# Issuing the paced conditioning loads from GpSimd instead of ScalarE in a two-layer diffusion backbone

## The chip, the core and the metric

The kernel runs on one core of one Trainium2 chip. The metric is device microseconds for one launch. Three runs of the kernel before gave 2462.93, 2460.25 and 2460.77 us (median 2460.77). One further execution was profiled: it took 2457.31 us, and the instructions in its trace span 2455.5 us.

The engines are named as the profile names them: PE (TensorE matmul) with PEld (its weight loads), DVE (VectorE), ACT (ScalarE), POOL (GpSimd) and SP (SyncE, which here only issues DMAs). Every engine runs its own instructions in the order that was fixed when the program was built.

## The reference

The model has two layers on 256 latent tokens (width 2048) with a prefix of 256 context tokens that is used in layer 0 only. Layer 0 mixes by attention (16 heads, a clamped 8 by 16 window of grid neighbours with a learned bias, and all context keys, in one softmax). Layer 1 mixes by a gated MLP with a 128 by 128 position matrix for each of 16 groups. A SwiGLU FFN of inner width 5632 follows each mixer. Cut to what matters:

```python
def ada_params(cond, w, b):
    return jnp.split(jax.nn.silu(cond) @ w + b, 6, axis=-1)
...
sh1, sc1, g1, sh2, sc2, g2 = ada_params(c[:, None, :], ada_w[i], ada_b[i])
a = modulate(h, sh1, sc1)                       # h * (1 + scale) + shift
...
h = layer_norm(ALPHA * h + g1 * y, ln_g[i, 0], ln_b[i, 0])
h = layer_norm(ALPHA * h + g2 * swiglu(modulate(h, sh2, sc2), ffn_w_in[i], ffn_w_out[i]),
               ln_g[i, 1], ln_b[i, 1])
```

For one conditioning vector, `silu(cond) @ w` is a product of a vector with a matrix of 2048 by 12288 in each layer. It has little arithmetic, but every byte of `ada_w` must come from memory. This document is about the loads of that matrix.

## The kernel before

**The matrix products.** Float32 operands are split into a high part `hi` and a rest `lo`, and each product is three matmuls (`mm3`, lines 89 to 91). Weights come in *pieces* of 128 by 1024 (512 KB): SP issues the load into one of four `raw` buffers, ACT casts it to `hi` (line 94, a tile `hw...`), and DVE subtracts to get `lo` (line 95, a tile `lw...`). In the FFN a product uses one piece for 12 matmuls of 512 columns, and up to five pairs of `hi` and `lo` exist, so four pieces can be ahead. In the attention stage there are three pairs, two ahead.

**The stages.** First come the modulated input, keys and values of the first heads (up to about 160 us), then the attention heads, the output projection, FFN of layer 0 (blocks named `pg`, `pu` and, for the way down, `pod`), the gated MLP (`gv`, `gu`, `pogo`), and FFN of layer 1.

**The paced conditioning work.** Most of `silu(c) @ ada_w` is not needed at once. It is cut into 320 tasks, each on one 128 by 1024 piece of `ada_w` (512 KB). A dot task (192 of them, load named `ad`, line 153) multiplies the piece by `silu(c)` and sums it along the row, for shifts and scales. A gate task (128 of them, load named `ag`, line 177) adds the scaled piece to a `gate` tile in place. Both are one DVE instruction, SCALAR_TENSOR_TENSOR. After 32 gate tasks a sum task has POOL add the `gate` tile over the partitions (line 192, PARTITION_ALL_REDUCE). `pace` and `tick` spread the tasks in the written program: after each piece, `tick` adds credit and runs as many tasks as it pays for. `fetch_ahead` writes the load of a task up to three tasks ahead of its use (`FETCH = 3`), and the loads share four buffers (`ADA = 4`), so a load waits until the DVE instruction of the task four before it is done.

**What sets the order.** A scheduler that builds the program takes the written instructions and fixes each engine's order. The written order is the priority, but an instruction that the scheduler takes to be ready early may be placed early on its engine. `keep_in_program_order` adds one rule: the instruction stays behind the instruction that was written just before it for the same engine. It says nothing on other engines.

POOL has little else to do: four memsets of `gate` tiles with a small DMA each (lines 171 and 172), the four sums of line 192, and broadcasts of norm rows over the partitions (line 83), each of which waits for a small SP load.

Of the kernel before, what the change touches and what calls it, by code (L numbers as in the profile page):

```python
# [52 lines left out]
def hybrid_kernel(ctx: ExitStack, tc: tile.TileContext, i, out):  # L53
    nc = tc.nc
# [20 lines left out]

    def load(src, name):
        r = outer.tile([P, 1024], F32, tag="ada", name=name, bufs=ADA)
        tc.keep_in_program_order(nc.scalar.dma_start(r, src))
        return r

    def spread(dst, src):
# [61 lines left out]
    def dot_task(layer, t, nt, half):  # L143
        key = (layer, t, nt, half)

        def fetch():
            src = i["ada_t"][dot_index(layer, t, nt)]
            loaded[key] = load(src[:, half * 1024 : (half + 1) * 1024], f"ad{layer}{t}{nt}{half}")

        def run():  # L150
            r = loaded.pop(key)
            o = (cols2 if half else cols)[:, layer, t, :]
            V.scalar_tensor_tensor(  # L153
                r, r, 1.0, c_bc[:, half * 1024 : (half + 1) * 1024], ALU.mult, ALU.mult,
                accum_out=o[:, nt : nt + 1],
            )
            if nt == KT - 1 and half:
                o = cols[:, layer, t, :]
                V.tensor_tensor(o, o, cols2[:, layer, t, :], ALU.add)
                V.tensor_tensor(o, o, badj[:, layer, t, :], ALU.add)  # L160
        return [(layer, t), 0.5, run, fetch]

    def gate_task(layer, t, kt, half):
        key = (layer, t, kt, half)
        sl = slice(half * 1024, (half + 1) * 1024)

        def fetch():
            if kt == 0 and half == 0:
                g = outer.tile([P, D], F32, tag="gate", name=f"gate{layer}{t}")
                gate[(layer, t)] = g  # L170
                nc.gpsimd.memset(g, 0.0)
                nc.gpsimd.dma_start(g[0:1, :], i["ada_b_row"][layer, t : t + 1, :])
            loaded[key] = load(i["ada_g"][gate_index(layer, t, kt)][:, sl], f"ag{layer}{t}{kt}{half}")

        def run():
            g = gate[(layer, t)][:, sl]
            V.scalar_tensor_tensor(g, loaded.pop(key), c_col[:, kt, 0:1], g, ALU.mult, ALU.add)  # L177
        return [(layer, t), 0.5, run, fetch]
# [826 lines left out]
```

## Time and profile before

| | |
|---|---|
| median of three runs | 2460.77 us (2460.25 to 2462.93) |
| profiled execution | 2457.31 us |
| span of its instructions | 2455.5 us |
| busy share of PE, DVE, ACT, POOL | 97%, 71%, 46%, 5% |
| moved by DMA | 610.57 MB, mean 249 GB/s |
| of that by SP's queue q1, by ACT's queue q10 | 440.64 MB, 167.89 MB |
| granted TensorE clock | 0.994 |

The profile page gives busy time per engine, the span in 40 slices, the DMA queues, the chain of work that ended last and the costliest groups of instructions. Behind it the trace can be asked for one window, one line or one engine: for the instructions in order of time, for groups of them (busy time, mean, and the idle time of the engine just before them with what ended it), and for who waited for whom. Idle time of an engine that is not the bottleneck costs nothing, so the first question to each row is whether PE had to wait for it.

To speak of places, the DVE instructions that split weight pieces (line 95, tiles `lw...`) are numbered in their order on DVE, 1 to 732, which is the same order before and after the change. The table gives the start of a few of them in the trace of before.

| weight piece split on DVE, number | 14 | 70 | 140 | 228 | 490 | 510 |
|---|---|---|---|---|---|---|
| starts at, us (before) | 160.1 | 455.7 | 728.3 | 970.9 | 1758.1 | 1812.5 |
| stage | attention begins | attention | FFN 0 | FFN 0 | FFN 1 | FFN 1 |

### The profile page before, as it was taken

Reading aid. Unit: us, or ns where it says so; the run is one execution under the profiler, and the core shown is the slowest. Engines: PE = TensorE matmul, PEld = TensorE weight load, DVE = VectorE, ACT = ScalarE, POOL = GpSimd, SP = SyncE. Lnnn points to the kernel's source line nnn. Section 1 sums busy time; section 2 is a strip of 40 time slices with the busy share of each in tenths; the row PEclk is TensorE's granted clock in tenths of the full one; section 3 lists DMA queues with packets and bytes.
Section 4 is the critical chain, followed back from the end, with each engine's and each line's share of the span. In section 5 each row is a group of like instructions: output and inputs, shape, how many; then the busy total and the mean of one; then the engine's idle time right before and its main releaser. Section 6 shows DMA issues by size and latency. Waiting matters only on the chain. (4 is left out here: it accounts for less than half of the span.)

```text
span 2455.5 us, 31276 instructions
## 1 busy us (share of the span) xinstructions
PE 2381.3 (97%) x11574; PEld 1975.5 (80%) x11574; DVE 1754.1 (71%) x2159; ACT 1121.0 (46%) x1534; POOL 111.4 (5%) x56
## 2 busy tenths in 40 slices
PE   6999899999999999999999999999999999999998
PEld 5788788888778888888788878777888888888886
DVE  3878877777887776666778788778755555566666
ACT  3344434345554444444455464446544444445553
POOL 0000200000010020000000010020100000020000
PEclk9999999999999999999999999999999999999999
DMA  8978787877568888888888767766666667766563
GB/s 332 350 261 264 241 286 266 271 260 252 185 229 293 298 270 295 287 288 290 275 287 280 275 203 261 256 213 198 209 226 227 227 225 228 227 198 193 176 212 131
DMA packets 167394, 610.57 MB, mean 249 GB/s; under 512 B 18916, under 2 KB 21284, under 8 KB 162884
## 3 DMA queue, kind: packets, MB, share of 16 engines
q1 hardware_dynamic: 120888, 440.64, 54.1%
q10 hardware_dynamic: 46224, 167.89, 19.8%
q8 instruction: 90, 1.47, 0.2%
q14 instruction: 64, 0.52, 0.1%
q0 software_dynamic: 128, 0.03, 0.0%
HBM read 606.40 MB, written 2.10 MB: 248 GB/s over the span
## 5 line engine op out<-in xcount | busy, mean ns | idle before, releaser
L94 ACT CAST hwf<-rwf 128x1024 fp32r<-128x1024 f32 x320 | 337.0, 1054 | 491.5 <-PE pu L91 203.3
L95 DVE TENSOR_TENSOR lwf<-rwf,hwf 128x1024 fp32r<-128x1024 f32 x320 | 405.2, 1279 | 167.9 <-ACT hwf L94 166.8
L153 DVE SCALAR_TENSOR_TENSOR ad<-ad,c_bc 128x1024 f32<-128x1024 f32 x192 | 233.9, 1222 | 172.3 <-DMA ad<-in_ada_t 171.8
L89 PE MATMUL pod<-hwd,ghd 128*128 128x512 f32 x684 | 267.1, 390 | 4.1 <-DVE sg L783 4.1
L91 PE MATMUL pod<-hwd,gld 128*128 128x512 f32 x684 | 266.8, 391 | 0.5 <-DVE gld L95 0.5
L90 PE MATMUL pod<-lwd,ghd 128*128 128x512 f32 x684 | 266.5, 390 | 0.0
L95 DVE TENSOR_TENSOR lwd<-rwd,hwd 128x1024 fp32r<-128x1024 f32 x172 | 211.8, 1232 | 53.1 <-ACT hwd L94 52.9
L177 DVE SCALAR_TENSOR_TENSOR gate<-ag,c_col,gate 128x1024 f32<-128x1024 f32 x128 | 164.6, 1290 | 116.0 <-DMA ag<-in_ada_g 115.2
L94 ACT CAST hwd<-rwd 128x1024 fp32r<-128x1024 f32 x172 | 180.4, 1049 | 28.2 <-PE pu L91 13.0
L89 PEld LDWEIGHTS pod<-hwd,ghd 128*128 128x128 f32 x684 | 128.7, 188 | 31.2 <-DVE sg L783 4.6
L91 PEld LDWEIGHTS pod<-hwd,gld 128*128 128x128 f32 x684 | 128.6, 188 | 27.9 <-DVE gld L95 0.9
L90 PEld LDWEIGHTS pod<-lwd,ghd 128*128 128x128 f32 x684 | 128.7, 188 | 26.4
L89 PE MATMUL pg<-hwf,f1h 128*128 128x512 f32 x320 | 126.4, 395 | 0.0
L89 PE MATMUL pg<-hwf,f0h 128*128 128x512 f32 x320 | 126.4, 395 | 0.0
L91 PE MATMUL pg<-hwf,f1l 128*128 128x512 f32 x320 | 124.7, 390 | 0.0
L91 PE MATMUL pg<-hwf,f0l 128*128 128x512 f32 x320 | 124.7, 390 | 0.0
L89 PE MATMUL pu<-hwf,f0h 128*128 128x512 f32 x320 | 124.5, 389 | 0.0
L90 PE MATMUL pu<-lwf,f0h 128*128 128x512 f32 x320 | 124.5, 389 | 0.0
L91 PE MATMUL pu<-hwf,f0l 128*128 128x512 f32 x320 | 124.5, 389 | 0.0
L89 PE MATMUL pu<-hwf,f1h 128*128 128x512 f32 x320 | 124.5, 389 | 0.0
L90 PE MATMUL pu<-lwf,f1h 128*128 128x512 f32 x320 | 124.5, 389 | 0.0
L91 PE MATMUL pu<-hwf,f1l 128*128 128x512 f32 x320 | 124.5, 389 | 0.0
(341 smaller groups left out, 5332.0 us busy)
## 6 DMA issues: line engine op xcount, KB each, us to landing
rwf<-in_w_in_t SPq DMA_DIRECT2D x320, 512.0 KB
ad<-in_ada_t ACTq DMA_DIRECT2D x192, 512.0 KB
rwd<-in_w_out SPq DMA_DIRECT2D x176, 512.0 KB
ag<-in_ada_g ACTq DMA_DIRECT2D x128, 512.0 KB
rwg<-in_w_gin SPq DMA_DIRECT2D x64, 512.0 KB
ap<-in_ada_p SPq DMA_DIRECT2D x19, 1024.0 KB
rwq<-in_w_q SPq DMA_DIRECT2D x32, 512.0 KB
rwo<-in_w_o SPq DMA_DIRECT2D x32, 512.0 KB
```

The lines of the kernel that those rows point to most:

```text
L89: keep(T.matmul(ps, sh, mh, start=first, stop=False))
L90: keep(T.matmul(ps, sh, ml, start=False, stop=False))
L91: keep(T.matmul(ps, sl, mh, start=False, stop=last))
L94: S.copy(hi, src)
L95: V.tensor_tensor(lo, src, hi.bitcast(F32), ALU.subtract)
L153: V.scalar_tensor_tensor(r, r, 1.0, c_bc[:, half * 1024 : (half + 1) * 1024], ALU.mult, ALU.mult, accum_out=o[:, nt : nt + 1],)
L177: V.scalar_tensor_tensor(g, loaded.pop(key), c_col[:, kt, 0:1], g, ALU.mult, ALU.add)
```

## The change

The load of a conditioning piece is issued by GpSimd and no longer by ScalarE. Nothing else in the source differs.

```diff
     def load(src, name):
         r = outer.tile([P, 1024], F32, tag="ada", name=name, bufs=ADA)
-        tc.keep_in_program_order(nc.scalar.dma_start(r, src))
+        tc.keep_in_program_order(nc.gpsimd.dma_start(r, src))
         return r
```

The rule of `keep_in_program_order` now holds against POOL's written order, and the scheduler, run on the changed source, fixes other orders on PE, DVE, ACT, SP and POOL.

**ACT and POOL in the FFN of layer 0.** The piece `lwf0031_0` is one of the split pieces of FFN 0. Names: `hwf`, `rwf` are the cast and the raw weight piece, `ag` and `ad` are conditioning pieces of gate and dot tasks. On ACT before, each load stands behind the casts written ahead of it:

```order
L78 DMA ag0591_7093<-in_ada_g 128x1024
L94 CAST hwf0123_0_7097<-rwf0123_0_7095 128x1024
L94 CAST hwf0123_1024_7115<-rwf0123_1024_7113 128x1024
L78 DMA ag05100_7132<-in_ada_g 128x1024
L94 CAST hwf0030_0_7136<-rwf0030_0_7134 128x1024
L94 CAST hwf0030_1024_7154<-rwf0030_1024_7152 128x1024
L78 DMA ag05101_7171<-in_ada_g 128x1024
```

On POOL with the change, the loads of the same stage follow one another, with the sum of line 192 (ISA) between them:

```order
L78 DMA ag05150_7526<-in_ada_g 128x1024
L78 DMA ag05151_7569<-in_ada_g 128x1024
L78 DMA ad1100_7657<-in_ada_t 128x1024
L78 DMA ad1101_7696<-in_ada_t 128x1024
L192 ISA gate05_6273<-gate05_6273 128x2048
L78 DMA ad1110_7741<-in_ada_t 128x1024
L78 DMA ad1111_7780<-in_ada_t 128x1024
```

Before, two casts of weight pieces stood between two loads. With the change, what holds a load back on its engine is only the loads, sums and broadcasts of POOL and the buffer that it needs.

**DVE in the FFN of layer 0.** The same stretch of weight pieces on DVE, before:

```order
L95 TENSOR_TENSOR lwf0122_0_7059<-rwf0122_0_7056,hwf0122_0_7058 128x1024
L95 TENSOR_TENSOR lwf0122_1024_7077<-rwf0122_1024_7074,hwf0122_1024_7076 128x1024
L95 TENSOR_TENSOR lwf0123_0_7098<-rwf0123_0_7095,hwf0123_0_7097 128x1024
L177 SCALAR_TENSOR_TENSOR gate05_6273<-ag0591_7093,c_col_58,gate05_6273 128x1024
L95 TENSOR_TENSOR lwf0123_1024_7116<-rwf0123_1024_7113,hwf0123_1024_7115 128x1024
```

and with the change:

```order
L95 TENSOR_TENSOR lwf0122_0_7059<-rwf0122_0_7056,hwf0122_0_7058 128x1024
L153 SCALAR_TENSOR_TENSOR ad1130_7879,cols_74<-ad1130_7879,c_bc_101 128x1024
L95 TENSOR_TENSOR lwf0122_1024_7077<-rwf0122_1024_7074,hwf0122_1024_7076 128x1024
L153 SCALAR_TENSOR_TENSOR ad1131_7922,cols2_75<-ad1131_7922,c_bc_101 128x1024
L153 SCALAR_TENSOR_TENSOR ad1140_7967,cols_74<-ad1140_7967,c_bc_101 128x1024
L95 TENSOR_TENSOR lwf0123_0_7098<-rwf0123_0_7095,hwf0123_0_7097 128x1024
L153 SCALAR_TENSOR_TENSOR ad1141_8012,cols2_75<-ad1141_8012,c_bc_101 128x1024
L95 TENSOR_TENSOR lwf0123_1024_7116<-rwf0123_1024_7113,hwf0123_1024_7115 128x1024
```

Between the same four weight pieces stand four conditioning tasks where one stood, and they are later tasks: `ad1130` belongs to layer 1. Counted over the whole order of DVE, so many of the 320 tasks stand ahead of a weight piece:

| ahead of weight piece number | 14 | 70 | 96 | 140 | 228 | 371 | 490 | 510 |
|---|---|---|---|---|---|---|---|---|
| before | 0 | 88 | 127 | 133 | 179 | 253 | 291 | 295 |
| with the change | 0 | 126 | 128 | 135 | 254 | 256 | 294 | 319 |

## The prediction

> **What bounds the kernel now.** I read the page's engine line first, then a table of windows, then who waits for whom on PE and on DVE.
>
> ```profile
> PE 2381.3 (97%) x11574; PEld 1975.5 (80%) x11574; DVE 1754.1 (71%) x2159; ACT 1121.0 (46%) x1534; POOL 111.4 (5%) x56
> ```
>
> PE is busy for 97% of the span, so nearly every microsecond that PE is made to wait is added to the time, and little can be won back. The windows show where other engines come near to it (after the window and its length: busy us and instructions of each engine, granted clock, DMA share, GB/s):
>
> ```profile
> core 0: us, PE busy (x) PEld busy (x) DVE busy (x) ACT busy (x) POOL busy (x), PEclk, DMA share, GB/s
> 10.00:30.00 20.00, 7.57 (x98) 5.92 (x91) 2.62 (x8) 7.87 (x10) 4.76 (x3) 1.00 1.02 415
> 60.00:140.00 80.00, 79.64 (x599) 63.41 (x598) 68.47 (x91) 30.45 (x53) 0.00 (x0) 1.00 0.96 348
> 160.00:456.00 296.00, 282.30 (x1600) 246.24 (x1599) 235.37 (x339) 127.07 (x212) 12.78 (x1) 0.99 0.80 266
> 728.00:971.00 243.00, 243.00 (x1097) 201.37 (x1097) 175.18 (x169) 104.41 (x115) 12.77 (x1) 1.00 0.85 290
> 1758.00:1813.00 55.00, 55.00 (x249) 45.48 (x249) 34.68 (x35) 24.96 (x30) 0.80 (x1) 1.00 0.71 236
> ```
>
> The last three windows are the stretches of the table of weight pieces: attention (pieces 14 to 70), FFN 0 (140 to 228) and FFN 1 (490 to 510). In FFN 0 PE never stops, while DVE has 68 us to spare and the DMA engines run at 0.85. The waits on PE and DVE over the whole span:
>
> ```profile
> PE pt L520 <- ACT p L510: 14.0, 7, 6.3
> PE pod L89 <- DVE sg L783: 4.1, 1, 4.1
> ...
> DVE ad L153 <- DMA ad<-in_ada_t: 171.8, 101, 5.0
> DVE lwf L95 <- ACT hwf L94: 166.8, 138, 2.0
> DVE gate L177 <- DMA ag<-in_ada_g: 115.2, 74, 4.6
> ```
>
> No wait of PE names a conditioning load. DVE stands 287 us (171.8 + 115.2) before conditioning tasks, but the pieces that it has split ahead cover that. So PE sets the time, and DVE's idle time is a reserve that the pacing leaves free.
>
> **The change part by part.** *What is removed.* ACT loses the issue of 320 loads:
>
> ```profile
> L78 ACTq DMA_DIRECT2D ad<-in_ada_t x192: 334/334/1498, 260.9 to 1377.7; - x192
> L78 ACTq DMA_DIRECT2D ag<-in_ada_g x128: 334/335/1377, 164.0 to 2153.3; - x128
> ```
>
> That is 320 x 0.334 = 107 us of an engine that is 46% busy. The one large wait of PE on ACT is 14.0 us (`pt`, in attention). The gain lies between 0 and those 14 us; I take 4, because a chain through DVE and PE ends at the same place.
>
> *What is moved.* A load loses its place behind ACT's casts. The orders show that with this the pacing goes too: the scheduler puts the conditioning tasks on DVE as early as it believes their loads to be there. Ahead of piece 70 stand 126 tasks instead of 88, between pieces 140 and 228 there are 119 instead of 46, and between 490 and 510 there are 25 instead of 4. DVE works in order, so a weight piece has to wait for all tasks ahead of it, and each of those for its load. The stretches get 38, 73 and 21 tasks more, which are missing in later stretches where PE already ran without a gap; that relief brings nothing back. The cost per task is one DVE instruction and one load (after the bar: busy us, mean ns, and the idle time before with what ended it):
>
> ```profile
> L95 DVE TENSOR_TENSOR lwf<-rwf,hwf 128x1024 fp32r<-128x1024 f32 x320 | 405.2, 1279 | 167.9 <-ACT hwf L94 166.8
> L153 DVE SCALAR_TENSOR_TENSOR ad<-ad,c_bc 128x1024 f32<-128x1024 f32 x192 | 233.9, 1222 | 172.3 <-DMA ad<-in_ada_t 171.8
> L177 DVE SCALAR_TENSOR_TENSOR gate<-ag,c_col,gate 128x1024 f32<-128x1024 f32 x128 | 164.6, 1290 | 116.0 <-DMA ag<-in_ada_g 115.2
> ...
> ad<-in_ada_t ACTq DMA_DIRECT2D x192, 512.0 KB
> ```
>
> In busy time a task is 1.22 us (233.9/192) or 1.29 us (164.6/128), and 0.524 MB; the first row is the split of a weight piece, 1.27 us (405.2/320).
>
> *FFN 0.* DVE: 175.2 + 73 x 1.22 = 264 us of work against 243 us of PE. DMA: 290 GB/s x 243 us = 70.5 MB, and 73 x 0.524 = 38.3 MB more, 108.8 MB. At 415 GB/s, the highest rate in the windows above, this takes 262 us; at 348 GB/s, the highest that is held for long, 312 us. The second is perhaps no limit, since PE was 99.6% busy there and asked for no more, so the two are the bounds. A third limit is the four buffers, shown by one load and the task that uses it:
>
> ```profile
> 796.80 0.34 ACTq L78 DMA_DIRECT2D ag<-in_ada_g  x1
> ...
> 803.80 1.29 DVE L177 SCALAR_TENSOR_TENSOR gate<-ag,c_col,gate 128x1024 f32<-128x1024 f32 x1 [2.02 <-DMA ag<-in_ada_g]
> ```
>
> From issue to landing are 7.0 us, and a buffer is free again 1.3 us later. Four buffers give one load in (7.0 + 1.3)/4 = 2.1 us, so 119 loads need 250 us. Three limits of 250 to 312 us that hold each other up (DVE stands while a load is late, the next load starts only after DVE) do not reach the best of them. I take 300 us, nearer to the held rate: +57, bounds +19 and +69.
>
> *Attention.* DVE: 235.4 + 38 x 1.22 = 282 us against 282.3 us of PE in a window of 296. DMA: 266 x 296 = 78.7 MB plus 19.9 is 98.6 MB, 238 us or 283 us at the two rates. All three just fit, but DVE there also waits for others in its order (below) and prefetch is two pieces deep, so not all of it fits. Lower bound 0. Upper bound: DVE's 282, the load waits that it has there now (33.4 + 15.4 = 49) and its waits for ACT and PE (11): 342, +46. I take +25.
>
> ```profile
> DVE ad L153 <- DMA ad<-in_ada_t: 33.4, 22, 3.5
> DVE gate L177 <- DMA ag<-in_ada_g: 15.4, 12, 2.7
> DVE lwq L95 <- ACT hwq L94: 5.2, 4, 2.4
> DVE s L503 <- PE s L91: 3.2, 4, 2.1
> DVE lwv L95 <- ACT hwv L94: 2.4, 3, 1.3
> ```
>
> *FFN 1.* DVE: 34.7 + 21 x 1.29 = 62 us against 55. DMA: 236 x 55 = 13.0 MB plus 11.0 is 24.0 MB, 58 us or 69 us. Bounds +3 and +14; I take +9.
>
> *What the moved loads queue behind.* On POOL they stand behind the sum of line 192, and only two loads stand between the last gate load and the first sum:
>
> ```profile
> 863.20 13.55 DVE L95 TENSOR_TENSOR lwf<-rwf,hwf 128x1024 fp32r<-128x1024 f32 x4
> 863.38 12.77 POOL L192 PARTITION_ALL_REDUCE gate<-gate  x1 [140.96 <-DVE gate L177]
> ```
>
> The next load starts when the sum ends, 12.8 us later, and takes the 7.0 us from above. The row of DVE shows that four weight splits take 13.55 us under the sum instead of 4 x 1.27, so DVE loses most of that time already. The third task of the next kind then stands until about 20 us after the last gate task, and behind it stand weight splits.
>
> In FFN 0 four pieces of cover are 4 x 243/88 = 11 us, when they are full. For the two sums with loads close behind them (attention and FFN 0) the cost is 0 to 9 us each; I take 4 each, +8.
>
> *POOL's own issue.* The trace has one form of DMA from POOL, 16 runs of 512 bytes on one partition:
>
> ```profile
> L172 POOL DMA_DIRECT2D gate<-in_ada_b_row x4: 500/509/832, 155.0 to 1710.9; - x4
> ```
>
> A conditioning load has 128 rows. The lower bound is the same 0.5 us; the upper, if it grows with the runs, 8 x 0.51 = 4.1 us. I take about 1 us, nearer to the lower end since the bytes are not POOL's to move; that is below the 2.1 us per load and costs nothing more. The other end is a rival.
>
> By the Trainium skill (DMA: Bandwidth & Descriptors, "Anatomy of one DMA — SWDGE (gpsimd) path") descriptor generation is small and a DMA from GpSimd takes about 2.0 us plus its bytes at 436 GB/s; an estimate from that page is 3.2 us for 512 KB, and the sum by it would be the one below. No run here shows it yet.
>
> *Sum* against the profiled execution of 2457.3 us: -4 + 57 + 25 + 9 + 8 = +95, 2552 us. The median of the three runs shown is 3.5 us above that execution, so I predict 2556 us.
>
> **The rivals.**
>
> *Not slower: the reserve absorbs it.* DVE's 287 us of load waits shrink, as POOL issues as soon as a buffer is free; the sum of line 192 is hidden, and 4 to 14 us of PE's waits on ACT go: about 2450 us. It decides if FFN 0 stays at 243 us. Against it, that needs 108.8/243 = 448 GB/s, above the 415 GB/s seen at best, and 264 us of DVE work in 243.
>
> By the Trainium skill (DMA: Bandwidth & Descriptors, "Issuing engines are not separate DMA queues") the choice of issuing engine saves only the issue time, as all DMAs run on the same 16 engines. That is this rival's time; the orders above are why I do not follow it.
>
> *Slower, but only by the hard limits.* DMA runs at 415 GB/s and DVE without gaps: FFN 0 +21 (264 - 243), FFN 1 +7 (62 - 55), the rest 0: 2457 + 28 = 2485, as a median 2489. For it: in the window of 60 to 140 us PE was 99.6% busy at 348 GB/s, so near-full queues need not hurt.
>
> *POOL is the bound.* At 4.1 us for an issue the stretches take 119, 126 and 25 times 4.1 us: 488, 517 and 103 instead of 243, 296 and 55, in all +514: 2971 us. Against it is only the small row of 0.5 us.
>
> *POOL's issue holds DVE up.* Under the sum DVE lost 13.55 - 4 x 1.27 = 8.5 of 12.77 us, two thirds. If an issue of 1 us does the same, the 270 tasks of the three stretches cost 270 x 0.67 = 181 us more on DVE, which is then the bound: FFN 0 takes 264 + 119 x 0.67 = 344, attention 282 + 84 = 366, FFN 1 62 + 17 = 79, so +101, +70 and +24: 2652 us, as a median 2656. Against it, a weight split ran in its usual time under the one kind of issue that there is:
>
> ```profile
> 673.64 1.19 DVE L95 TENSOR_TENSOR extra_o<-rwt,extra_o 128x1024 fp32r<-128x1024 f32 x1
> ...
> 673.67 0.52 POOL L172 DMA_DIRECT2D gate<-in_ada_b_row  x1 [0.30 <-POOL gate L171]
> ```
>
> The Trainium skill (SBUF — State Buffer, "SBUF: two separate sides") has a DVE instruction with two SBUF inputs blocked only by a GpSimd instruction that reads SBUF. The rows of the sum and of this issue agree with it.
>
> *The change does not do what it says:* excluded, the orders show the loads on POOL.
>
> **How the numbers follow.** Chances: the forecast 0.65, the hard limits alone 0.15, POOL's issue holding DVE 0.08, POOL as the bound 0.06, the reserve absorbs it 0.06. The forecast's own range is 2500 (FFN 0 at 264, attention +10, FFN 1 +7, sums 0) to 2610 (upper bounds of all but one). For 8 in 10 I go to 2485, which leaves out the first rival and some of the second, and to 2640, which leaves out the two on POOL's issue. A measurement tells 0.2% (5 us) from no change. Faster by more than that: 0.04 (the reserve absorbs it, and PE's waits on ACT go). Within it: 0.02. Slower: 0.94, all the other cases.
>
> **What would show it.** In the profile after: FFN 0's stretch (weight pieces 140 to 228) lasts about 300 us, with DMA share above 0.95 and DVE above 85%; PE has new waits for `lwf` or `hwf`, and pieces 228 to 371 are untouched. POOL's issue has a mean of about 1 us and DVE's SCALAR_TENSOR_TENSOR keeps 1.2 to 1.3 us. The prediction is wrong if FFN 0 stays at 243 us, if PE waits chiefly where no tasks were added, or if POOL is busy without a gap in FFN 0.

## The result, and the profile after

The change makes the kernel slower: the median goes from 2461.85 us (four runs, 2460.25 to 2466.84, on the same chip) to 2536.47 us (four runs, 2527.78 to 2539.98). The ratio is 1.0275, with a 95% interval of 1.0251 to 1.0298, so +75 us on the medians. The profiled execution of the changed kernel took 2539.98 us with a span of 2538.2 us at a granted clock of 0.985; against the profiled execution of before that is +83 us. What follows compares these two traces.

The engine line and the DMA queues of the page after:

```profile
PE 2408.8 (95%) x11574; PEld 1984.0 (78%) x11574; DVE 1768.8 (70%) x2159; ACT 1120.7 (44%) x1534; POOL 272.1 (11%) x376
...
q1 hardware_dynamic: 120888, 440.64, 52.0%
q0 software_dynamic: 46208, 167.83, 18.5%
```

The loads have moved to POOL's queue q0 with all their bytes. POOL's busy share doubles and stays small. PE falls from 97% to 95% of a longer span: it has about 55 us more idle time, and 27 us more busy time for the same 11574 matmuls.

The windows of the stretches that the prediction set out from, moved to where the same weight pieces (14 to 70, 140 to 228, 490 to 510) now lie (columns as in the prediction):

```profile
160.00:477.00 317.00, 290.35 (x1598) 250.82 (x1597) 280.66 (x418) 128.31 (x211) 78.13 (x125) 0.97 0.89 310
748.00:1048.00 300.00, 264.65 (x1113) 208.23 (x1112) 260.28 (x322) 105.65 (x117) 74.06 (x119) 0.97 0.97 362
1832.00:1894.00 62.00, 58.84 (x261) 46.98 (x260) 57.13 (x51) 24.06 (x29) 12.14 (x23) 1.00 1.00 380
```

FFN 0 takes 300 us where it took 243. PE is idle for 35 of them, the DMA engines are full (0.97), and DVE is busy for 87%. The bytes agree with this: 108.8 MB at 362 GB/s are 300 us. The waits over the whole span, after:

```profile
DVE ad L153 <- DMA ad<-in_ada_t: 59.9, 68, 4.9
...
PE pu L90 <- DVE lwf L95: 34.5, 20, 7.6
...
DVE gate L177 <- DMA ag<-in_ada_g: 28.3, 29, 2.9
...
PE sp L849 <- DVE u L850: 13.3, 2, 7.4
```

DVE's idle time before conditioning loads shrinks from 287 to 88 us, as one could wish. It is traded for new waits of PE on split weight pieces (`lwf`). Those in turn go back to the raw pieces, as the waits inside FFN 0 (748 to 1048 us) show:

```profile
ACT hwf L94 <- DMA rwf<-in_w_in_t: 169.5, 72, 10.0
...
DVE ad L153 <- DMA ad<-in_ada_t: 30.5, 43, 3.1
...
PE pu L90 <- DVE lwf L95: 25.5, 17, 7.6
```

ACT stands 169.5 us before loads of the weights themselves (54.0 us in the same stretch before), which the conditioning loads now crowd.

This table gives the length of each stage in the two profiled executions, from the first matmul of a stage to the first of the next.

| stage | before, us | after, us | difference |
|---|---|---|---|
| attention | 413.2 | 427.2 | +14.0 |
| output projection | 94.2 | 95.0 | +0.8 |
| FFN 0, up (`pg`, `pu`) | 493.7 | 549.7 | +56.0 |
| FFN 0, down (`pod`) | 250.1 | 243.3 | -6.8 |
| gated MLP, `gv` | 95.5 | 91.9 | -3.6 |
| gated MLP, `gu` | 100.8 | 111.2 | +10.4 |
| gated MLP, `pogo` | 97.1 | 95.3 | -1.8 |
| FFN 1, up | 493.8 | 507.6 | +13.8 |
| FFN 1, down | 240.5 | 240.4 | -0.1 |

Two thirds of the loss lie in FFN 0, and about 12 us come back in the three stages whose tasks were moved away.

### The profile page after: what moved, and what is told of

The parts are those of the page before. It is cut to its first block, busy times and chain, and to the rows that moved or that the text cites. A ratio compares the mean times of both kernels' runs of the same rounds, so it can differ in the third digit from the quotient of the medians.

```text
span 2538.2 us, 31634 instructions
## 1 busy us (share of the span) xinstructions
PE 2408.8 (95%) x11574; PEld 1984.0 (78%) x11574; DVE 1768.8 (70%) x2159; ACT 1120.7 (44%) x1534; POOL 272.1 (11%) x376
## 5 line engine op out<-in xcount | busy, mean ns | idle before, releaser
L153 DVE SCALAR_TENSOR_TENSOR ad<-ad,c_bc 128x1024 f32<-128x1024 f32 x192 | 240.9, 1267 | 60.8 <-DMA ad<-in_ada_t 59.9
L94 ACT CAST hwd<-rwd 128x1024 fp32r<-128x1024 f32 x172 | 180.2, 1048 | 17.7 <-PE pu L91 16.6
L177 DVE SCALAR_TENSOR_TENSOR gate<-ag,c_col,gate 128x1024 f32<-128x1024 f32 x128 | 163.3, 1286 | 29.6 <-DMA ag<-in_ada_g 28.3
L90 PE MATMUL pu<-lwf,f0h 128*128 128x512 f32 x320 | 129.6, 405 | 26.5 <-DVE lwf L95 26.5
L78 POOL DMA_DIRECT2D ad<-in_ada_t x192 | 101.3, 528 | 343.2 <-DVE ad L153 321.6
L90 PE MATMUL pg<-lwf,f0h 128*128 128x512 f32 x320 | 126.0, 394 | 4.1 <-DVE lwf L95 4.1
```

Source lines behind the costliest of these rows:

```text
L78: tc.keep_in_program_order(nc.gpsimd.dma_start(r, src))
L90: keep(T.matmul(ps, sh, ml, start=False, stop=False))
L94: S.copy(hi, src)
L153: V.scalar_tensor_tensor(r, r, 1.0, c_bc[:, half * 1024 : (half + 1) * 1024], ALU.mult, ALU.mult, accum_out=o[:, nt : nt + 1],)
```

## The experiments

Each experiment is compared with the kernel before, run on its own chip: a median of 2472.34 us (seven runs) for the first four kernels and 2467.17 us (eleven runs) for the other four. "Stretch" is the time between the starts of weight pieces 140 and 228 on DVE.

The theory was that the loss is one of order: without its pacing, the conditioning work is packed into the stretches where DMA and DVE have too little left. The rivals are the path over POOL itself, DVE's work, the bytes, and the sums of line 192.

### The loads on POOL, with the DVE tasks kept in the written order

```diff
-            V.scalar_tensor_tensor(
+            pin(V.scalar_tensor_tensor(
...
-            V.scalar_tensor_tensor(g, loaded.pop(key), c_col[:, kt, 0:1], g, ALU.mult, ALU.add)
+            pin(V.scalar_tensor_tensor(g, loaded.pop(key), c_col[:, kt, 0:1], g, ALU.mult, ALU.add))
```

`pin` is the kernel's own name for `keep_in_program_order`. The load stays on POOL; only the instruction that uses it is held at its written place.

> Loads stay on GpSimd, but the DVE instruction of each conditioning task is kept behind the instruction written before it for DVE, so that the tasks stand on DVE where the pacing wrote them (87 tasks ahead of weight piece 70, 46 between pieces 140 and 228, 3 between 490 and 510; the kernel before has 88, 46 and 4, the change 126, 119 and 25). Theory (lost pacing: the tasks crowd DVE and the DMA engines): the loss goes, 2450 to 2475 us, FFN 0's stretch 243 us. Rival (the path over POOL itself: later landing, issue on POOL, loads queued behind the sums): more than half of the +75 us stays, above 2495 us.

Measured: 2445.56 us (2443.84 to 2447.53), ratio 0.9887 [0.9872, 0.9902]. The window of FFN 0, and the waits over the span:

```profile
716.00:961.00 245.00, 244.93 (x1104) 202.50 (x1103) 177.07 (x165) 106.19 (x116) 35.53 (x46) 1.00 0.84 290
```

```profile
DVE ad L153 <- DMA ad<-in_ada_t: 4.2, 3, 1.8
...
DVE gate L177 <- DMA ag<-in_ada_g: 0.5, 1, 0.5
```

FFN 0 is back at 245 us with PE busy throughout, at the DMA share and rate of before. The loads over POOL come in time: DVE waits for them less than 5 us in all. So the path over POOL costs nothing; the loss is in the order. The time is a little below the expected 2450 to 2475 us, since the pins bring a gain of their own, which the next run measures.

### The loads on ACT, with the DVE tasks kept in order

The same two `pin` lines on the kernel before. It separates what the pins bring from what POOL brings.

> The kernel before (loads on ScalarE) with the same rule for the tasks' DVE instructions: the control for that rule. Both theories: 2455 to 2475 us. Against p1 it gives the price of the path alone, ACT or POOL, at one DVE order: theory within 8 us of p1, rival p1 slower by 35 us or more.

Measured: 2451.89 us (2450.52 to 2454.59), ratio 0.9911 [0.9894, 0.9927]. The pins alone bring 20 us against the kernel before, and POOL in place of ACT a further 6 us (2451.89 - 2445.56). The intervals of the two ratios still overlap, but the runs themselves don't (2450.52 to 2454.59 against 2443.84 to 2447.53, on one chip). What the change was about, the issuing engine, is thus worth about 6 us once the order is held, and its sign is the other one.

The Trainium skill (DMA: Bandwidth & Descriptors, "Issuing engines are not separate DMA queues") states that loads run on the same 16 DMA engines whichever engine issues them, and that issuing from several engines saves only the issue time. These 6 us, beside 107 us of issue time that ACT is spared, agree with it for the path. It does not touch the 75 us that come from the order.

### The loads on ACT, without their pacing

```diff
-        tc.keep_in_program_order(nc.scalar.dma_start(r, src))
+        nc.scalar.dma_start(r, src)
```

Here POOL has no part in the loads, and they lose their place behind the casts.

> The kernel before with the loads on ScalarE, but no longer kept in program order. The scheduler then lets tasks run ahead as in the change, though less (102 tasks ahead of piece 70, 94 between 140 and 228, 23 between 490 and 510). Theory (lost pacing): slower, by the tasks added about 57 x 48/73 = 37 us in FFN 0, 5 in attention, 13 in FFN 1: 2505 to 2525 us, more if loads that wait for a buffer hold up ACT. Rival (the path over POOL): stays at 2455 to 2470 us, since POOL issues nothing.

Measured: 2516.82 us (2506.16 to 2521.51), ratio 1.0169 [1.0141, 1.0197]. Between pieces 140 and 228 stand 94 tasks (46 before, 119 with the change), and the stretch takes 266.7 us:

```profile
739.00:1006.00 267.00, 253.18 (x1102) 206.13 (x1101) 229.85 (x278) 105.60 (x117) 13.91 (x1) 0.97 0.96 357
```

With about two thirds of the extra tasks the kernel loses 44 us, as expected, without any load on POOL. By the prediction's counting this stretch moves 70.5 + 48 x 0.524 = 95.7 MB, and 95.7 MB in 267 us are 358 GB/s, beside the 357 of the row, at a share of 0.96. Again the DMA engines are nearly full. ACT could also be held up by its own loads, which wait for a free buffer; in this window waits of its casts that end with a task or with a conditioning load come to at most 19 us of 267.

### The changed kernel, with a sixteenth of the bytes

```diff
-        tc.keep_in_program_order(nc.gpsimd.dma_start(r, src))
+        tc.keep_in_program_order(nc.gpsimd.dma_start(r[:, 0:64], src[:, 0:64]))
...
-                r, r, 1.0, c_bc[:, half * 1024 : (half + 1) * 1024], ALU.mult, ALU.mult,
+                by64(r)[:, 1:16, :], r[:, None, 0:64].to_broadcast([P, 15, 64]), 1.0,
+                by64(c_bc[:, half * 1024 : (half + 1) * 1024])[:, 1:16, :], ALU.mult, ALU.mult,
...
-            g = gate[(layer, t)][:, sl]
-            V.scalar_tensor_tensor(g, loaded.pop(key), c_col[:, kt, 0:1], g, ALU.mult, ALU.add)
+            g = by64(gate[(layer, t)][:, sl])
+            r = loaded.pop(key)[:, None, 0:64].to_broadcast([P, 16, 64])
+            V.scalar_tensor_tensor(g, r, c_col[:, kt, 0:1], g, ALU.mult, ALU.add)
```

`by64` only views a row as sixteen parts of 64. Each load brings 64 of 1024 columns, and DVE reads them again and again, so DVE's work stays (960 columns in a dot task, 1024 in a gate task) and most of the bytes go. 15 of 16 conditioning columns are left out of the computation.

> The change with a sixteenth of the bytes in each conditioning load (64 of 1024 columns, which DVE then reads over and over; a dot task works on 960 columns instead of 1024, so the results are not the reference's). The order on DVE stays that of the change (120 tasks between 140 and 228). If late transfers make the rest above DVE's own work (38 us of load waits in FFN 0, 35 in attention, 12 in FFN 1): FFN 0 about 255 us instead of 300, total 2470 to 2495 us. If DVE's work alone sets it: FFN 0 near 290, total above 2515 us.

Measured: 2444.08 us (2443.31 to 2444.9), ratio 0.9881 [0.9866, 0.9896], below the expected time. The stretch takes 253.7 us with 120 tasks in it; this window covers nearly all of it:

```profile
716.00:965.00 249.00, 245.34 (x1091) 200.36 (x1090) 245.53 (x323) 104.06 (x114) 74.64 (x117) 0.99 0.63 194
```

DVE is busy for 98.6% of the window, and PE hardly notices: it is idle for 3.7 us. So DVE's crowding, one of the prediction's three limits, costs little here: the way up of FFN 0 takes 501.6 us from first matmul to first matmul, against 494.6 with the tasks in their written order and 549.7 with the change. The DVE stretch itself is 11 us longer than before (253.7 against 242.6), about the four pieces that had been split ahead. The smaller loads also land sooner (2.8 us instead of 6.9), so this run relieves the four buffers together with the DMA engines. It doesn't tell these two apart.

### The changed kernel, with an eighth of DVE's work

```diff
-                r, r, 1.0, c_bc[:, half * 1024 : (half + 1) * 1024], ALU.mult, ALU.mult,
+                r[:, 0:W8], r[:, 0:W8], 1.0, c_bc[:, half * 1024 : half * 1024 + W8], ALU.mult, ALU.mult,
...
-            g = gate[(layer, t)][:, sl]
-            V.scalar_tensor_tensor(g, loaded.pop(key), c_col[:, kt, 0:1], g, ALU.mult, ALU.add)
+            g = gate[(layer, t)][:, half * 1024 : half * 1024 + W8]
+            V.scalar_tensor_tensor(g, loaded.pop(key)[:, 0:W8], c_col[:, kt, 0:1], g, ALU.mult, ALU.add)
```

With `W8 = 128` all bytes are loaded, and a task works on 128 of its 1024 columns; the rest is left out of the computation.

> The change with full loads, but each conditioning task's DVE instruction works on 128 of its 1024 columns (the results are not the reference's). DVE has about 1.1 us less per task; the scheduler packs the tasks still closer (104 of them between weight pieces 140 and 200, where the change has 81). If bytes decide: 164 pieces of 0.524 MB are 86 MB, at the 362 GB/s that the change reached in FFN 0 237 us for 60 weight pieces instead of 166, and the total is 2520 to 2560 us. If DVE's work decides: FFN 0 as before, total 2440 to 2475 us.

Measured: 2586.69 us (2583.9 to 2592.09), ratio 1.0487 [1.0459, 1.0515]. It is slower than the change itself and slower than expected. A window in FFN 0:

```profile
750.00:1050.00 300.00, 250.45 (x1039) 193.82 (x1038) 154.48 (x336) 97.19 (x107) 81.38 (x129) 0.97 0.95 362
```

DVE is busy for half the time only, and PE idles more than with the change (50 us against 35 in 300). With shorter tasks the scheduler packs them closer still: 104 tasks stand between pieces 140 and 200, where the change has 81, and ahead of piece 50 stand 106 in place of 75. So the order is not quite the change's, and the run is no measure of what DVE's work is worth in that order. But pieces 140 to 200 took 229.4 us, near the 237 us that were worked out from bytes alone. Together with the kernel with few bytes (nearly all of DVE's work and few bytes cost little; all bytes and little of DVE's work cost more) this points to one cause: the bytes bunched in front of the weight pieces make most of the loss, not DVE's instructions.

### The changed kernel without the sums of line 192

```diff
-            nc.gpsimd.partition_all_reduce(g, g, P, ReduceOp.add)
+            pass
```

The gates are left without their sum over the partitions. The change itself was run once more on the same chip.

> The change without the four sums over partitions on GpSimd (line 192; the gates are then not the reference's). The order on DVE is that of the change. In the change's profile PE waited 7.8 us in FFN 0, 7.8 us in the gated MLP and 6.8 us in FFN 1 where a sum ran, and 5 to 9 us in attention. If the sums cause these waits: 22 to 30 us less than the change, about 2510 us. If they only cover a delay that the loads cause anyway: within 8 us of the change.

> The change once more, on the chip of the other three, to measure them against it: 1.025 to 1.030 of the kernel before.

Measured: without the sums 2510.15 us (2502.32 to 2513.57), ratio 1.0179 [1.0148, 1.0209]; the change again 2532.14 us (2530.63 to 2544.1), ratio 1.0274 [1.0243, 1.0304]. So the sums cost 22 us in the changed order, as expected. The stretch in FFN 0 takes 281.5 us without and 296.1 us with them, which is 14.6 us. The window without the sums:

```profile
740.00:1021.00 281.00, 259.00 (x1118) 204.70 (x1117) 250.74 (x321) 105.68 (x117) 62.27 (x118) 0.99 1.01 387
```

Here the DMA engines carry 387 GB/s for 281 us, at a share of 1.01. With the engines full throughout, 108.8 MB take 281 us; so neither the four buffers nor DVE set the time here. (A stretch of 65 us in the kernel with little DVE work reached 400 GB/s, so 387 need not be the very limit.) The rest, up to 296 us here and 300 in the first trace of the change, comes with the sum. How it does so is to be seen in that trace, in order of time (start and duration, then in brackets the idle time before):

```profile
810.35 11.88 POOL L192 PARTITION_ALL_REDUCE gate<-gate  x1 [4.48 <-DVE gate L177]
...
810.56 10.00 DVE L153 SCALAR_TENSOR_TENSOR ad<-ad,c_bc 128x1024 f32<-128x1024 f32 x1 [0.30 <-DMA ad<-in_ada_t]
...
820.49 1.22 DVE L95 TENSOR_TENSOR lwf<-rwf,hwf 128x1024 fp32r<-128x1024 f32 x1
...
821.76 0.79 PE L90 MATMUL pu<-lwf,f0h 128*128 128x512 f32 x1 [7.65 <-DVE lwf L95]
...
822.12 2.11 POOL L78 DMA_DIRECT2D ad<-in_ada_t  x4
```

One conditioning task that starts under the sum takes 10.00 us on DVE instead of 1.22; the weight split behind it starts at 820.49, and PE has waited 7.65 us. The transfers stop too. While DVE stands, it frees neither a raw weight buffer nor a conditioning buffer, and POOL is in the sum, so the four loads of the last row come only behind it. In a stretch that is short of DMA time, the DMA engines do nothing for 8 us:

```profile
814.00:822.00 8.00, 0.35 (x2) 0.25 (x2) 8.00 (x4) 2.65 (x4) 8.00 (x1) 0.79 0.00 2
```

These 8 us are more than half of the 14.6. Before the change up to four pieces were split ahead when the sum came; at 863 to 877 us the DMA rate fell as well, to 153 GB/s, but PE did not stop. With the DMA engines full, there is no such stock. In the kernel with few bytes PE waits only 1.87 us at this sum. DVE and PE stand in the same way at the sums of the gated MLP (PE waits 7.42 us at 1656.8) and of FFN 1 (6.59 us at 1907.1, with the DMA engines at 2 GB/s from 1899 us on). The wait in the gated MLP seems not to hang on the bytes, as the kernel with few bytes has it too (6.73 us).

The waits also slow PE behind them. Rows of windows just after that wait of 7.65 us (the granted clock is the third number from the end):

```profile
822.50:824.00 1.50, 1.50 (x5) 1.17 (x4) 1.50 (x4) 0.00 (x0) 1.50 (x4) 0.50 0.84 202
...
825.50:827.00 1.50, 1.50 (x8) 1.25 (x7) 0.00 (x0) 0.18 (x1) 0.00 (x0) 0.99 0.95 279
```

The clock is 0.50 until about 825.3 us, and matmuls start every 0.43 us instead of 0.23. Over the whole stretch 34 matmuls are so spaced and cost 7 us, beside 41 us in 33 longer gaps (both counted from the starts of the matmuls). The Trainium skill (TensorE: Matmul & The Clock Gate, "What's actually happening") describes a monitor that halves the clock after an idle window of about 3.4 us and restores it after a busy one; the 3.5 us at 0.50 agree with this. The other four drops of the clock in this stretch did not need an idle window. Each followed 3.4 us in which PE was busy for 1.3 to 1.5 us, with one wait of 1.8 to 2.4 us. These two rows show one such stretch of 3.4 us, with a wait of 1.8 us in it, and the one behind it:

```profile
859.67:863.08 3.41, 1.35 (x8) 0.74 (x7) 3.41 (x6) 1.23 (x2) 0.53 (x1) 1.00 1.01 407
863.08:866.50 3.42, 3.42 (x9) 2.65 (x9) 3.42 (x5) 0.86 (x1) 0.53 (x1) 0.50 1.02 402
```

So a wait of about 2 us could halve the clock here as well as a long one; on this the measurement differs from the page.

### The last sum earlier, with the loads on POOL and the tasks in order

With the loads on POOL and the tasks in order (the first experiment) one wait of 7.7 us was left: PE in front of the way down of FFN 1, behind the last sum, which came just ahead of it.

```profile
PE pod L89 <- DVE sg L783: 7.7, 1, 7.7
```

```diff
-    pace(170)
+    pace(150)
```

`pace` is the written program's rate; with the smaller number the last tasks, and the sum behind them, come earlier.

> The version with loads on GpSimd and tasks kept in program order (p1), with the last 33 tasks spread over 150 units instead of 170, so that the last sum falls inside FFN 1's blocks and not at the way down, where PE waited 7.9 us under it. If that wait is the sum's and four split pieces cover it: 2436 to 2441 us, 0.9835 to 0.987 of the kernel before. If not, p1's 0.989 stays.

Measured: 2436.46 us (2432.8 to 2440.53), ratio 0.9876 [0.9855, 0.9898]. The last sum starts at 2126.3 us and not at 2181.9, the wait before the way down is gone, and the way down of FFN 1 takes 240.5 us in the trace against 250.7. The ratio can't be told from the 0.9887 without this edit, which was run on another chip, so a gain in the whole time isn't shown. The version as a whole is 31 us faster than the kernel before.

## Why the prediction was right, and where it was not

**Direction, place and cause hold.** Slower was forecast, with the order on DVE and not POOL as the cause. FFN 0's stretch was to go from 243 to 300 us: it measures 299.7. DMA share above 0.95 (0.97), DVE above 85% (87%), PE's new waits on `lwf`, and landing in about 7.0 us (6.9 for `ad`, 7.2 for `ag`) came as described. The total was to be 2556 us within 2485 to 2640; it is 2536.

**The 300 us of FFN 0 are right by two errors that cancel, which is luck.** The step said that three limits (DVE's 264 us, the bytes' 262 to 312, the buffers' 250) hold each other up. The runs show one of them: with few bytes a full DVE costs PE little, and with little DVE work the bytes cost as much or more. And without the sum the stretch takes 281 us, with the DMA engines full at 387 GB/s, not 300; the "held rate" of 348 GB/s, to which the choice leaned, was no limit, as its own sentence feared. The sum of line 192 fills the gap: 14.6 us in this stage, where the prediction took 4 on top of the 300.

**The term of the sums was mis-sized.** The prediction took +8, four each in attention and FFN 0. Taking the sums out brings 22 us. In the two traces of one chip, with and without them, the way up of FFN 0 differs by 17.9 us, `gu` of the gated MLP by 8.3, the way up of FFN 1 by 3.6 and attention by 2.3. The gated MLP and FFN 1 weren't in the term at all. It looked only for loads queued behind a sum on POOL, while what hurts is the DVE instruction that is caught under it with no split pieces in stock, and in FFN 0 the DMA engines that stand still meanwhile.

**Attention was over-sized:** +25 was taken, PE measures +14.0. On DVE the stretch of pieces 14 to 70 grew by 20.8 us, but 7 of them came back by piece 96. **FFN 1** was to cost +9, within +3 and +14, and cost +13.8. The stretch of pieces 490 to 510 grew by 6.5 us (54.4 to 60.9). PE waits 6.59 us under the sum behind it, but taking the sums out shortens this stage by 3.6 us only (507.7 to 504.1), so about 10 us stay for the order.

**"That relief brings nothing back" was wrong.** It failed because PE had small waits there after all. The way down of FFN 0, `gv` and `pogo` became 12 us shorter together; PE's idle time in the three fell from 12.1 to 4.2 us, and two stretches of 3.4 us at half clock went with it. Pieces 228 to 371, which were to be untouched, went from 399.8 to 387.0 us. Between +95 and the measured +83 in the profiled executions, this term (-12), attention (-11) and FFN 0 (-5: 57 and 4 were taken, 56 measured) take away, and `gu` (+10) and FFN 1 (+5) add; the output projection makes up the rest.

**POOL's issue** takes 0.527 us with 128 rows, not about 1, and so hardly more than with one partition's 16 runs (0.50). The rival of 4.1 us falls. This group row of after shows it:

```profile
L78 POOL DMA_DIRECT2D ad<-in_ada_t x192 | 101.3, 528 | 343.2 <-DVE ad L153 321.6
```

What it waits for is DVE, that is, a free buffer. The landing times stand in the page's list of DMA issues:

```profile
ad<-in_ada_t POOLq DMA_DIRECT2D x192, 512.0 KB, 6.9
...
ag<-in_ada_g POOLq DMA_DIRECT2D x128, 512.0 KB, 7.2
```

The rival by which the issue holds DVE up falls too:

```profile
L153 DVE SCALAR_TENSOR_TENSOR ad<-ad,c_bc 128x1024 f32<-128x1024 f32 x192 | 240.9, 1267 | 60.8 <-DMA ad<-in_ada_t 59.9
L177 DVE SCALAR_TENSOR_TENSOR gate<-ag,c_col,gate 128x1024 f32<-128x1024 f32 x128 | 163.3, 1286 | 29.6 <-DMA ag<-in_ada_g 28.3
```

The mean of a gate task is unchanged (1286 ns against 1290); that of a dot task is up by 45 ns, 8.6 us over 192, which is about the one task of 10.00 us under the sum.

**The hard limits alone (2489) fell for a reason that its own text did not see.** It put FFN 0 at DVE's 264 us with DMA at 415 GB/s. DVE was no limit, and 415 GB/s were not held: 387 are the most that a whole stretch of FFN 0 kept up. And it took nothing for the sums, which cost 22 us. **The reserve absorbs it (2450)** fell as argued: it needed 448 GB/s. The measured times of the two kernels with pinned tasks are near its figure, but by pacing, not by taking the tasks early.

**ACT's issue** was to bring 4 us. With the order held, POOL in place of ACT brings 6 us, inside the 0 to 14 that were given.

What stays open: why the pinned tasks make even the kernel with the loads on ACT 20 us faster than before. Its waits of DVE on conditioning loads go from 287 to 6 us, and that is a likely cause, but no run takes it apart. The traces (of two chips) point to attention, which takes 401.6 us against 413.2, with PE idle for 9.0 us and not 18.1.

## What to carry to other kernels

When a side load moves to another engine, look first at the order that comes out, not at the engine: here a rule on the load had paced the work through the casts ahead of it, and the path itself was worth 6 us against 75 lost to the order. If side work has to be spread, hold the instruction that uses the data at its place, not only the load. Count in bytes, and not by the DMA share, what a stretch has to spare. FFN 0 ran at 290 GB/s and a share of 0.85, and 387 GB/s is what it kept up with the engines full. In its 243 us that leaves room for 45 more pieces; 73 came, and what is beyond is paid in PE's time even when other engines have room. Where a long reduction on POOL is near, keep split pieces in stock for as long as it lasts.

## What the runs showed of the hardware that was not expected

- A load of 512 KB in 128 rows occupies POOL for 0.527 us, hardly more than one of 16 short runs (0.50).
- Queues of POOL and SP with 512 KB loads keep up 362 to 387 GB/s over 280 to 300 us, at a DMA share of 0.95 to 1.01. The share is not in proportion to the rate: 290 GB/s showed as 0.85.
- One sum over the partitions (11.88 to 12.80 us) stretches a single DVE instruction to 10.0 us, a conditioning task (10.00) as well as a weight split (9.67 and 10.14 us at the other sums). In FFN 0 the DMA engines then stood still for 8 us.
- PE's wait of 7.65 us was followed by about 3.5 us at half the granted clock, so that a wait costs more than its own length. A wait of 1.8 us, with PE busy for 1.35 of 3.4 us around it, did the same.
